# One layer of a hybrid encoder on one core: branch B's output chunks moved to the values' bank ring, a third home for its gates, finer key loads, and branch A's chunks with the rings swapped

## The chip, the core and the metric

The kernel runs on 1 core of one Trainium2 chip. A core has five engines that each follow an own list of instructions: TensorE (PE, with its weight loads shown as PEld), VectorE (DVE), ScalarE (ACT), GpSimd (POOL) and SyncE (SP, which here only issues DMAs). The metric is the device time of one execution in microseconds. The kernel before was run three times: 1937.47, 1938.02 and 1940.12 us, median 1938.02 us.

## The reference, cut to what matters

```python
D_MODEL = 1024; SEQ = 1024; HEAD_DIM = 64; NA_HEADS = 8; NB_HEADS = 8; NB_KV_HEADS = 2
GRID_W = 64; NA_KH_MAX = 8; NA_KW = 16; WIN = 128; BLOCK = 128; D_FF = 2816

h = x + 0.5 * swiglu(rms_norm(x, ffn1_norm), w_gate1, w_up1, w_down1)
u = rms_norm(h, mix_norm)
qA, kA, vA, qB, kB, vB, gA, gB = jnp.split(u @ w_in, SPLITS, axis=-1)
yA = neighbourhood_attention_2d(qA, kA, vA, na_rpb)                # 8 heads of 64
yB = windowed_gqa_sink(rope(qB), rope(kB), vB, sink_logit)         # 8 heads, 2 key heads
h = h + (sigmoid(gA) * (yA @ w_branch_a) + sigmoid(gB) * (yB @ w_branch_b)) @ w_out
h = h + 0.5 * swiglu(rms_norm(h, ffn2_norm), w_gate2, w_up2, w_down2)
out = rms_norm(h, final_norm)                                      # all float32
```

The line that the change touches is the sum of the two gated branches, and the attention that feeds it. `yA` and `yB` are 1024 tokens by 512; each branch's product with its 512x1024 weight is made in eight chunks of 128 output columns, transposed, so that a chunk is 128 partitions by 1024 tokens: two PSUM banks of 128x512. The gates `gA` and `gB` are likewise eight chunks of 128x1024 each.

## The kernel before, in words

**The whole.** In order of time: the first FFN, the input projection, an attention stage, the product with `w_out` (called the merge here), the second FFN, the last norm. Every float32 product with 512 columns is three TensorE matmuls in reduced precision, made by `mm3` (high part by high part, high by low, low by high: L149, L151 and L153), from operands that were split into a high part by an ACT cast (L95) and a low part by a DVE subtraction (L98).

**The attention stage** is a software pipeline over 64 units (`scores`, `turn`, `values`, lines 1364 to 1420). Units n = 0 to 31 are branch B (8 query blocks by 4 pairs of heads), units 32 to 63 are branch A (4 pairs of heads `hp` by 8 query blocks `j`). In step n the PE does the scores of unit n (L1379, L1380, two banks), the transposes of unit n-1's probabilities (L1398, two banks) and the product with the values of unit n-2 (L1412 for A, L1417 for B, one bank). Between them DVE and ACT make the softmax (L1382 on DVE, which also takes the score's bank out of PSUM; L1385, L1390 on ACT), the split of the transposed probabilities (L95, L98), and `write`, which takes the values' bank out of PSUM (L1348 copy on ACT; L1349 and twice L1352 on DVE).

**The bank rings.** PSUM has 8 banks here, in two rings of four: ring d (scores, transposes, transposes of V) and ring g (values, and the filling work below). A tile that asks a ring for a bank gets one that is or first becomes free.

**The filling work.** Twice per step, `filling(n)` takes some steps of a generator `filler()` and so puts other matmuls between those of attention: first ten projections of gate chunks (`gate`, 8 steps each, two banks of ring g, copied out by ACT at L1208 and stored to HBM, `g_d`, by POOL at L1209), then `branch_b`, the eight chunks of branch B's product (4 steps of 6 matmuls each), then the first two chunks of branch A (`branch_a`); branch A's other chunks follow after the last unit. A chunk's two banks come from ring d for even and ring g for odd chunks in branch B, and the other way round in branch A. Some 1.7 steps are taken per unit up to unit 45, 1.6 up to 59, and 3 after.

**The gates' way.** A chunk of branch B needs its gate back from `g_d`: SP fetches it (`fetch_gate`, L1245, 512 KB) into a tile of tag `xs`, of which there are two; ACT opens it (`open_gate`, L1254, one tanh over 128x1024, fixed in its place in ACT's order by `pin`); DVE evicts the chunk's two banks (L1279, twice 128x512) with the gate as the other operand. The gate of chunk dc+1 is asked for after the first step of chunk dc and opened at the end of chunk dc. The chunk's weights come by `fetch_w` (L1249, 512 KB) into a ring of tiles `ws`. The inputs `yB` come back from HBM by `fetch_y` (L1222) and are split in two by `split_y` (ACT and DVE, 128x1024, L95 and L98), four of them, during the steps of the last gate projection.

**Branch A's loads.** `prep_a(hp)` loads a pair of heads: per k two K tiles in high and low part, and the queries, by POOL (L1172, L1174, 256 KB each), then V by SP (L1177), and, some steps later, V's transposes (L1185, ring d) with their split into `fx`. It goes on by one `yield` at two places of each unit. The bias tables come by SP (L1157), the inner ones into parts of `fa`, the edge ones into `held[0..3]`, four of six tiles `hs`; `held[4]` and `held[5]` are not used. After blocks 3 and 7 of a pair of heads, POOL stores its `y` to `y_d` (L1357, 128x512), except for the last pair.

**The end of the stage.** After the last unit, branch A's chunks are evicted (L1518), added to branch B's (L1519), combined and stored (`combine`, L1495), and `Down(4, wo)`, the merge, begins: its first product takes the four banks of ring d, the second those of ring g.

**The order** of each engine's instructions is made when the kernel is built, by a scheduler that follows the program and its own estimate of durations; on the chip each engine takes its list in order and waits at semaphores. A DMA on SP or POOL that waits holds up those behind it.

## Time and profile before

| | us |
|---|---|
| median of 3 runs | 1938.02 (1937.47 to 1940.12) |
| the profiled execution | 1936.38 |
| its span, first to last instruction | 1934.6 |
| PE busy | 1916.3 (99%) |
| DVE busy | 1451.0 (75%) |
| ACT busy | 945.4 (49%) |
| POOL busy | 295.6 (15%) |
| granted TensorE clock, mean | 0.997 |

The profile comes from one profiled execution. Views of it that are used below: the page's head; the busy time of each engine in chosen stretches of time ("windows"); the chain of work that ended last, each piece with its start, its length and what it was; the waits, grouped by the engine and line that waited and what released it, with total, number and longest; the timeline of single instructions, where brackets give the idle time of the engine just before and what ended it; the groups of instructions of one line and shape, with number, total and mean; and the DMA issues with size and median time from issue to landing. `xs`, `ws`, `raw`, `fa`, `ar`, `fx` are tags of SBUF tiles, `d` and `g` the two rings of PSUM banks, `g_d`, `y_d`, `wab_d`, `zs_d`, `bm_d` tensors in HBM. On this time axis branch B's chunks run from 1081.33 us (first matmul) to 1170.46 us (end of the last eviction), and the merge's first matmul starts at 1213.43 us.

### The profile page before, as it was taken

To read this page: it belongs to the slowest core of one execution; us is meant where nothing else is said; L and a number is where in the kernel's file an instruction comes from. 1 tells how busy PE (TensorE), PEld (TensorE's weight loads), DVE (VectorE), ACT (ScalarE), POOL (GpSimd) and SP (SyncE) were. 2 spreads that over 40 slices of the span, in tenths; PEclk is the share of its full clock that TensorE was granted. 3 is DMA by queue.
4 is the path that set the end of the run, shared out by engine and by line. 5 is a ranking of instruction groups with operands and counts; after the bars stand their busy time and mean duration, and the time that the engine had idled before them with its cause. 6 is when DMAs were issued, how large, how long until landed. Compare 5 with 4: busy or idle time off the path is not lost.

```text
span 1934.6 us, 25628 instructions
## 1 busy us (share of the span) xinstructions
PE 1916.3 (99%) x8932; PEld 1597.9 (83%) x8932; DVE 1451.0 (75%) x2535; ACT 945.4 (49%) x1836; POOL 295.6 (15%) x454
## 2 busy tenths in 40 slices
PE   9999999999999999999999899999999999999998
PEld 7888888888888888888888788888888888888886
DVE  8987766768966878658778787989676566559864
ACT  7532444444446543447777774466333333344453
POOL 0011111214400112111122101010111001005210
PEclk9999999999999999999999999999999999999999
DMA  6254555586354267826357858443422323493341
GB/s 267 94 173 166 178 177 190 171 295 245 125 173 153 106 198 237 265 102 164 100 129 187 240 186 299 169 163 120 147 92 104 126 87 109 142 358 98 112 144 60
DMA packets 161344, 321.76 MB, mean 166 GB/s; under 512 B 16320, under 2 KB 69952, under 8 KB 161216
## 3 DMA queue, kind: packets, MB, share of 16 engines
q1 hardware_dynamic: 130048, 225.21, 35.8%
q0 software_dynamic: 30448, 93.87, 14.7%
q8 instruction: 70, 1.15, 0.2%
q10 hardware_dynamic: 720, 1.05, 0.1%
q14 instruction: 58, 0.48, 0.1%
HBM read 222.04 MB, written 99.81 MB: 166 GB/s over the span
## 4 chain that ended last, share of the span: by engine, by line
PE 95%; DVE 2%; ACT 1%; DMA 1%; issue 0%; SPq 0%; POOLq 0%; POOL 0%; DVEq 0%
PE g L149 17%; PE g L153 17%; PE g L151 17%; PE d L149 12%; PE d L153 12%; PE d L151 12%; PE d L1398 2%; PE g L1417 1%; PE d L1379 1%; PE d L1380 1%; PE g L1412 1%; DMA xs<-g_d 1%; PE d L142 1%; ACT fa L1385 0%; ACT ws L95 0%
## 5 line engine op out<-in xcount | busy, mean ns | idle before, releaser
L149 PE MATMUL g<-ar,ws 128*128 128x512 f32 x1096 | 414.8, 394 | 0.0
L151 PE MATMUL g<-ar,ws 128*128 128x512 f32 x1096 | 410.4, 390 | 0.0
L153 PE MATMUL g<-ar,ws 128*128 128x512 f32 x1096 | 409.6, 390 | 0.0
L149 PE MATMUL d<-ar,ws 128*128 128x512 f32 x760 | 293.2, 392 | 1.0 <-DVE nmx L1382 1.0
L151 PE MATMUL d<-ar,ws 128*128 128x512 f32 x760 | 292.9, 391 | 0.6 <-DVE ar L879 0.6
L153 PE MATMUL d<-ar,ws 128*128 128x512 f32 x760 | 291.9, 390 | 0.0
L153 PEld LDWEIGHTS g<-ar,ws 128*128 128x128 f32 x1096 | 205.6, 188 | 43.2
L151 PEld LDWEIGHTS g<-ar,ws 128*128 128x128 f32 x1096 | 205.5, 188 | 42.6
L149 PEld LDWEIGHTS g<-ar,ws 128*128 128x128 f32 x1096 | 201.2, 188 | 36.6 <-DVE fa L997 0.4
L322 DVE TENSOR_TENSOR ws<-raw,ws 128x512 fp32r<-128x512 f32 x210 | 143.9, 691 | 88.9 <-ACT ws L319 87.8
L319 ACT CAST ws<-raw 128x512 fp32r<-128x512 f32 x210 | 129.1, 621 | 145.6 <-PE g L153 64.5
L151 PEld LDWEIGHTS d<-ar,ws 128*128 128x128 f32 x760 | 142.9, 188 | 30.2 <-DVE ar L879 1.2
L149 PEld LDWEIGHTS d<-ar,ws 128*128 128x128 f32 x760 | 142.3, 188 | 30.9 <-DVE nmx L1382 1.2
L153 PEld LDWEIGHTS d<-ar,ws 128*128 128x128 f32 x760 | 142.8, 188 | 29.6 <-DVE ws L322 0.4
L95 ACT CAST ws<-raw 128x512 fp32r<-128x512 f32 (+1 forms) x107 | 70.7, 660 | 123.1 <-PE d L153 59.8
L98 DVE TENSOR_TENSOR ws<-raw,ws 128x512 fp32r<-128x512 f32 (+1 forms) x107 | 85.1, 795 | 46.0 <-ACT ws L95 45.9
L426 POOL DMA_DIRECT2D hid<-fx x91 | 49.4, 543 | 373.6 <-DVE fx L486 245.7
L98 DVE TENSOR_TENSOR ws<-ar,ws 128x512 fp32r<-128x512 f32 x114 | 94.1, 832 | 15.7 <-ACT ws L95 15.7
L95 ACT CAST ar<-raw 128x512 fp32r<-128x512 f32 (+1 forms) x81 | 54.1, 671 | 84.0 <-PE g L151 51.4
L1385 ACT ACTIVATE fa<-fa,nmx 128x385 f32<-128x385 f32 (+3 forms) x128 | 75.5, 591 | 33.7 <-DVE nmx L1382 32.0
L149 PE MATMUL g<-ws,ws 128*128 128x512 f32 x232 | 90.9, 392 | 0.0
L153 PE MATMUL g<-ws,ws 128*128 128x512 f32 x232 | 90.4, 390 | 0.0
(313 smaller groups left out, 3666.4 us busy)
## 6 DMA issues: line engine op xcount, KB each, us to landing
raw<-hid SPq DMA_DIRECT2D x70, 512.0 KB
hid<-fx POOLq DMA_DIRECT2D x91, 256.0 KB, 2.6
ar<-in_ffn_w_down_dram SPq DMA_DIRECT2D x32, 512.0 KB
raw<-in_ffn_w_up_dram SPq DMA_DIRECT2D x31, 512.0 KB
raw<-in_ffn_w_gate_dram SPq DMA_DIRECT2D x27, 512.0 KB
hid<-fa POOLq DMA_DIRECT2D x51, 256.0 KB, 2.7
raw<-in_w_in_dram SPq DMA_DIRECT2D x25, 512.0 KB
ar<-zs_d POOLq DMA_DIRECT2D x48, 256.0 KB, 7.0
```

The source lines that it names most:

```text
L95: hi = nc.scalar.copy(dst_hi, src)
L98: (eng or nc.vector).tensor_tensor(dst_lo, src, f32v(dst_hi), op=ALU.subtract)
L142: nc.tensor.transpose(pt[:, c * P:(c + 1) * P], xs[:, (half * 4 + c) * P:(half * 4 + c + 1) * P], ident)
L149: nc.tensor.matmul(b, lhs[0], r[0], start=first, stop=False, **kw)
L151: nc.tensor.matmul(b, lhs[0], r[1], start=False, stop=False, **kw)
L153: nc.tensor.matmul(b, lhs[1], r[0], start=False, stop=last, **kw)
L319: nc.scalar.copy(w[0][:, :512], a)
L322: nc.vector.tensor_tensor(w[0][:, 512:], a, f32v(w[0][:, :512]), op=ALU.subtract)
L426: nc.gpsimd.dma_start(hid[PRODUCTS.index(p), i], src)
L1379: nc.tensor.matmul(b[:, :nw], un["q"][s], un["kd"][s][:, k0 * P:k1 * P], start=True, stop=False)
L1385: nc.scalar.activation(pr, pr, AF.Exp, scale=-1.0, bias=nmx[:, s:s + 1], accum_out=ssum[:, s:s + 1])
L1398: nc.tensor.transpose(pt[:, i * P:(i + 1) * P], un["pr"][s][:, i * P:(i + 1) * P], ident)
```

## The change

It has six parts, all in the attention stage and the chunks beside it.

1. `branch_b` takes all its banks from ring g; before, its even chunks took ring d.
2. `branch_a` starts with ring d and goes on alternating, so its last chunk has its banks in ring g; before, in ring d.
3. The gates of branch B have three homes instead of two: gates 0, 3 and 6 go into `held[4]` and `held[5]`, in two DMAs of 128x512; the others into `xs`. A gate is asked for two chunks ahead (after the first step of chunk dc that of chunk dc+2, for chunk 0 after its third step); gates 0 and 1 are asked for during the last gate projection, at its steps 0 and 5. The tanh is two instructions of 128x512 per gate.
4. The third `split_y` of `yB` moves from step 5 to step 6 of the last gate projection, the fourth from step 6 of it into chunk 0, after its first step.
5. `prep_a` has one more `yield` after each of its four groups of K loads, so a pair of heads takes 13 steps of the generator instead of 9, and the transposes of V come two units later.
6. For the first three pairs of heads, `write` of branch A makes both heads' sum in one DVE instruction of 64x2x128 instead of two of 64x128, so `y` lies in 64 partitions with the two heads side by side, and is stored as 64x2x512.

The number of PE matmuls stays at 8932. DVE has 24 instructions fewer, ACT 8 more, SP 3 DMAs more.

```diff
             for lo, dst in enumerate((kd, kl)):
                 for a in halves(dst[k]):
                     nc.gpsimd.dma_start(a, head(k, 4, lo))
+                yield
...
     def branch_a(i):

-        bs = [bank("gd"[i % 2]) for _ in range(2)]
+        bs = [bank("dg"[i % 2]) for _ in range(2)]
...
     def fetch_gate(dc):
-        mix["rb", dc] = xs4()
-        nc.sync.dma_start(mix["rb", dc], g_d[D + dc * P:D + (dc + 1) * P, :])
+        t = xs4() if dc % 3 else None
+        mix["rb", dc] = [held[4 + k] if t is None else t[:, k * 512:k * 512 + 512] for k in range(2)]
+        for r, cols in zip(mix["rb", dc] if t is None else [t], (slice(0, 512), slice(512, 1024)) if t is None else (slice(0, 1024),)):
+            nc.sync.dma_start(r, g_d[D + dc * P:D + (dc + 1) * P, cols])
...
     def open_gate(dc):
-        r = mix["rb", dc]
-        pin(nc.scalar.activation(r, r, AF.Tanh, scale=0.5))
+        for r in mix["rb", dc]:
+            pin(nc.scalar.activation(r, r, AF.Tanh, scale=0.5))
...
         for dc in range(NC8):
-            bs = [bank("dg"[dc % 2]) for _ in range(2)]
+            bs = [bank("g") for _ in range(2)]
             mm = branch_mm(bs, mix.pop(("w", dc)), Y_B)
             for c in range(4):
                 drain(mm, 1)
                 yield
-                if c == 0:
+                if c == (0 if dc else 2) and dc + 2 < NC8:
+                    fetch_gate(dc + 2)
+                if c == 0 and dc == 0:
+                    split_y(Y_B[3], 3 * P, nc.vector)
+                if c == 1:
                     if dc == 0:
                         open_gate(0)
-                    if dc + 1 < NC8:
-                        fetch_gate(dc + 1)
-                elif c == 1:
                     fetch_w(dc + 2)
                 elif c == 3 and dc + 1 < NC8:
                     open_gate(dc + 1)
...
-                yield from gate(dc, {0: lambda: [fetch_y(c * P) for c in range(2)],
+                yield from gate(dc, {0: lambda: [fetch_gate(0)] + [fetch_y(c * P) for c in range(2)],
                                      1: lambda: fetch_w(0),
                                      2: lambda: fetch_y(2 * P),
                                      3: lambda: split_y(Y_B[0], 0, nc.vector),
                                      4: lambda: [split_y(Y_B[1], P, nc.vector), fetch_y(3 * P)],
-                                     5: lambda: [split_y(Y_B[2], 2 * P, nc.vector), fetch_gate(0)],
-                                     6: lambda: split_y(Y_B[3], 3 * P, nc.vector)})
+                                     5: lambda: fetch_gate(1),
+                                     6: lambda: split_y(Y_B[2], 2 * P, nc.vector)})
...
                     cols = slice((j - 3) * P, (j + 1) * P)
-                    if j in (3, 7) and hp == 3:
+                    if hp < 3:
+                        both = y[j // 4 * HD:j // 4 * HD + HD].rearrange("p (s t) -> p s t", s=2)
+                        nc.vector.tensor_tensor(both[:, :, j % 4 * P:(j % 4 + 1) * P], o[:HD, :, 0, :], lo, op=ALU.add)
+                        if j in (3, 7):
+                            nc.gpsimd.dma_start(y_d[512 + hp * P:512 + (hp + 1) * P, cols].rearrange("(s p) t -> p s t", s=2), both)
+                        return
```

Four places of the built order show it. The lines of the changed file are three to eight higher than those of the file before: the gates' fetch is L1245 before and L1248 after, the weights' L1249 and L1252, the `y` fetch L1222 and L1223, the tanh L1254 and L1257, the eviction of branch B L1279 and L1283, that of branch A L1518 and L1526, the transposes L1398 and L1406, the scores L1379, L1380 and L1387, L1388, ACT's part of the softmax L1385, L1390 and L1393, L1398, the copy of the values L1348 and L1352.

The first place is SP's list around branch B's first chunks. Before, `xs_9574` is gate 1, `xs_9711` gate 2, `xs_9856` gate 3, and `ws_9596`, `ws_9747` and `ws_9889` are the weights of chunks 2, 3 and 4:

```order
L1245 DMA xs_9574<-g_d 128x1024
L1157 DMA hs_6979<-bm_d 128x384
L1249 DMA ws_9596<-wab_d 128x1024
L1157 DMA hs_6980<-bm_d 128x384
L1249 DMA ws_9747<-wab_d 128x1024
L1245 DMA xs_9711<-g_d 128x1024
L1245 DMA xs_9856<-g_d 128x1024
L1222 DMA raw_10168<-y_d 128x1024
L1249 DMA ws_9889<-wab_d 128x1024
```

After, `xs_9630` is gate 2, the pair `hs_6981`, `hs_6982` (which are `held[4]` and `held[5]`) is gate 3, `xs_9843` gate 4, and `ws_9584`, `ws_9727`, `ws_9865` are the weights of chunks 2, 3 and 4:

```order
L1157 DMA hs_6979<-bm_d 128x384
L1157 DMA hs_6980<-bm_d 128x384
L1223 DMA raw_10092<-y_d 128x1024
L1248 DMA xs_9630<-g_d 128x1024
L1252 DMA ws_9584<-wab_d 128x1024
L1248 DMA hs_6981<-g_d 128x512
L1248 DMA hs_6982<-g_d 128x512
L1252 DMA ws_9727<-wab_d 128x1024
L1223 DMA raw_10152<-y_d 128x1024
L1248 DMA xs_9843<-g_d 128x1024
L1252 DMA ws_9865<-wab_d 128x1024
```

Gate 2 now stands ahead of the weights of chunk 2; the pair of gate 3, which goes where gate 0 was and so waits for chunk 0's eviction, stands ahead of the weights of chunk 3, which stood ahead of that wait before.

The second place is the PE's list where chunk 0 ends and chunk 1 begins. Before, chunk 0 is `d_9538`, `d_9539`, chunk 1 `g_9685`, `g_9686`, and `g_9649` is a unit's values:

```order
L153 MATMUL d_9538<-ar_5004,ws_9320 128x512
L1398 MATMUL d_9638<-ident,fa 128x128 x2
L153 MATMUL d_9539<-ar_5004,ws_9320 128x512
L1412 MATMUL g_9649<-ws_9582,fx_8927 128x256 x3
L1412 MATMUL g_9649<-ws_9583,fx_8928 128x256 x3
L1379 MATMUL d_9663<-ar_5003 128x384
L1380 MATMUL d_9663<-ar_563,ar_5003 128x384
L149 MATMUL g_9685<-ar_4625,ws_9536 128x512
L1379 MATMUL d_9668<-ar_5003 128x384
L1380 MATMUL d_9668<-ar_563,ar_5003 128x384
L149 MATMUL g_9686<-ar_4625,ws_9536 128x512
L151 MATMUL g_9685<-ar_4625,ws_9536 128x512
```

After, chunk 0 is `g_9517`, `g_9518`, chunk 1 `g_9670`, `g_9671`, and `g_9638` is a unit's values:

```order
L153 MATMUL g_9518<-ar_5004,ws_9309 128x512
L1420 MATMUL g_9638<-ws_9569,fx_9031 128x256 x3
L1387 MATMUL d_9651<-ar_5003 128x384
L1388 MATMUL d_9651<-ar_563,ar_5003 128x384
L149 MATMUL g_9670<-ar_4625,ws_9515 128x512
L151 MATMUL g_9670<-ar_4625,ws_9515 128x512
L1387 MATMUL d_9656<-ar_5003 128x384
L1388 MATMUL d_9656<-ar_563,ar_5003 128x384
L153 MATMUL g_9670<-ar_4625,ws_9515 128x512
L149 MATMUL g_9670<-ar_4625,ws_9515 128x512
L151 MATMUL g_9670<-ar_4625,ws_9515 128x512
L153 MATMUL g_9670<-ar_4625,ws_9515 128x512
```

Both chunks and the values are now in ring g, and chunk 1 runs ahead in its first bank; its second bank, `g_9671`, begins six rows further down, after one more matmul in the first and a unit's transposes.

The third place is ACT's list around the copies of the last gate projection's banks. Before, `fx_9400` is a cast of a V transpose of the third pair of heads, `ar_5004` the high parts of the last two splits of `yB`, `xs_9530` the gate that is copied out:

```order
L95 CAST fx_9400<-d_9447 128x4x64
L95 CAST ar_5004<-raw_9342 128x8x8x16
L1390 ACTIVATE fa<-fa,rc_9433 128x384
L95 CAST ws_9516<-d_9518 128x3x128
L1208 COPY xs_9530<-g_9231 128x512
L95 CAST ws_9517<-d_9524 128x3x128
L1208 COPY xs_9530<-g_9232 128x512
L1348 COPY s_771_6976<-g_9546 64x256
L1385 ACTIVATE fa,ssum_9493<-fa,nmx_9492 128x384 x2
L1390 ACTIVATE fa<-fa,rc_9494 128x384
L95 CAST ar_5004<-raw_9412 128x8x8x16
```

After, the copies of the last gate are a few rows ahead of this piece, and `raw_9333`, `raw_9393` are the third and fourth block of `yB`:

```order
L1398 ACTIVATE fa<-fa,rc_9462 128x384
L95 CAST ar_5004<-raw_9333 128x8x8x16
L95 CAST fx_9498<-d_9500 128x4x64
L1352 COPY s_771_6976<-g_9525 64x256
L1393 ACTIVATE fa,ssum_9536<-fa,nmx_9535 128x256 x2
L95 CAST fx_9498<-d_9551 128x4x64
L95 CAST fx_9499<-d_9500 128x4x64
L95 CAST ws_9568<-d_9570 128x3x128
L1398 ACTIVATE fa<-fa,rc_9537 128x256
L95 CAST fx_9499<-d_9551 128x4x64
L95 CAST ar_5004<-raw_9393 128x8x8x16
L95 CAST ws_9569<-d_9576 128x3x128
```

The third split of `yB` and the four casts of V, which stood ahead of the gate's copies, now stand behind them, among the work beside chunk 0. Each of these casts has a subtraction (L98) on DVE that follows it.

The fourth place is DVE's last evictions of branch A, chunks 6 and 7. Before:

```order
L1518 SCALAR_TENSOR_TENSOR raw_10753<-raw_10753,g_10829 128x512
L1518 SCALAR_TENSOR_TENSOR raw_10753<-raw_10753,g_10830 128x512
L1519 TENSOR_TENSOR ar_9534<-ar_9534,raw_10753 128x1024
L1495 TENSOR_TENSOR fa<-ar_9534 128x512
L1518 SCALAR_TENSOR_TENSOR raw_10788<-raw_10788,d_10860 128x512
L1518 SCALAR_TENSOR_TENSOR raw_10788<-raw_10788,d_10861 128x512
L1519 TENSOR_TENSOR ar_9535<-ar_9535,raw_10788 128x1024
```

After:

```order
L1526 SCALAR_TENSOR_TENSOR raw_10737<-raw_10737,d_10813 128x512
L1526 SCALAR_TENSOR_TENSOR raw_10737<-raw_10737,d_10814 128x512
L1527 TENSOR_TENSOR ar_9513<-ar_9513,raw_10737 128x1024
L1503 TENSOR_TENSOR fa<-ar_9513 128x512
L1526 SCALAR_TENSOR_TENSOR raw_10772<-raw_10772,g_10844 128x512
L1526 SCALAR_TENSOR_TENSOR raw_10772<-raw_10772,g_10845 128x512
L1527 TENSOR_TENSOR ar_9514<-ar_9514,raw_10772 128x1024
```

The last chunk's banks are now in ring g; those of ring d, which the merge takes first, are evicted one chunk earlier.

7 lines of the change are left out of this document (3 added, 4 removed).

## The prediction

> **What bounds the kernel.** I read the page's head first, then the chain of work that ended last, the waits, and stretches of the attention stage.
>
> ```profile
> span 1934.6 us, 25628 instructions
> PE 1916.3 (99%) x8932; PEld 1597.9 (83%) x8932; DVE 1451.0 (75%) x2535; ACT 945.4 (49%) x1836; POOL 295.6 (15%) x454
> ```
>
> PE is busy 1916.3 of 1934.6 us, and the change leaves its 8932 matmuls alone. So it can gain only from the 18.3 us in which PE idles, from matmuls that run at a lower clock, and from those that last longer than need be. The idle time by its causes, PE's waits first, then those of ACT and SP within 1030 to 1215 us:
>
> ```profile
> PE d L1398 <- DVE nmx L1382: 6.4, 1, 6.4
> PE d L149 <- DVE raw L1518: 1.1, 1, 1.1
> PE d L149 <- DVE nmx L1382: 1.0, 1, 1.0
> ACT xs L1254 <- DMA xs<-g_d: 7.0, 1, 7.0
> SPq L1245 <- DVE ar L1279: 26.2, 4, 9.3
> ```
>
> Three single waits of PE stand in the stretch that the change touches, 8.5 us of the 18.3. The longest belongs to a chain, here with start and length of each piece:
>
> ```profile
> 1094.60 14.76 DMA xs<-g_d
> 1109.39 1.06 ACT xs L1254
> 1110.44 0.51 ACT fa L1390
> 1112.32 0.90 PE d L1398 x3
> ```
>
> The timeline shows how the DMA came to be late:
>
> ```profile
> 1085.59 0.32 SPq L1245 DMA_DIRECT2D xs<-g_d  x1
> 1090.45 0.32 SPq L1249 DMA_DIRECT2D ws<-wab_d  x1
> 1093.86 0.67 DVE L1279 SCALAR_TENSOR_TENSOR ar<-xs,d 128x512 f32<-128x512 f32 x1
> 1094.50 1.05 ACT L1254 ACTIVATE xs<-xs 128x1024 f32<-128x1024 f32 x1
> 1094.60 10.02 SPq L1245 DMA_DIRECT2D xs<-g_d  x2
> 1109.39 1.06 ACT L1254 ACTIVATE xs<-xs 128x1024 f32<-128x1024 f32 x1 [6.99 <-DMA xs<-g_d]
> 1112.32 0.90 PE L1398 MATMUL d<-ident,fa 128*128 128x128 f32 x3 [6.45 <-DVE nmx L1382]
> ```
>
> Gate 1 (issued at 1085.59) was in before its tanh at 1094.50, which waited for nothing. Gate 2 could go only when DVE had evicted chunk 0 (1093.86 + 0.67) and so freed the tile; it needed 14.76 us. Its tanh is pinned in ACT's order, so the softmax of the next unit stood behind it: ACT idled 6.99 us, PE 6.45 us. The stretches around it:
>
> ```profile
> core 0: us, PE busy (x) PEld busy (x) DVE busy (x) ACT busy (x) POOL busy (x), PEclk, DMA share, GB/s
> 1069.00:1081.30 12.30, 11.20 (x71) 9.40 (x69) 10.90 (x28) 10.97 (x25) 0.00 (x0) 1.00 0.63 213
> 1081.30:1093.20 11.90, 11.87 (x69) 10.03 (x69) 11.02 (x39) 10.78 (x28) 5.83 (x11) 1.00 0.94 253
> 1093.20:1105.90 12.70, 12.67 (x71) 10.70 (x69) 10.24 (x30) 7.96 (x21) 2.12 (x4) 1.00 1.23 277
> 1105.90:1115.60 9.70, 3.28 (x11) 2.75 (x12) 3.09 (x10) 4.15 (x10) 0.00 (x0) 0.65 0.60 223
> 880.00:1020.00 140.00, 139.84 (x822) 122.86 (x821) 106.94 (x337) 109.63 (x285) 21.60 (x39) 1.00 0.50 126
> ```
>
> In the fourth stretch the granted clock is 0.65, and PE's 3.28 us there, all behind the stall, did about half of what such a time does elsewhere: a second price of the same stall.
>
> **The gains.** (1) Gate 2 is now asked for two chunks ahead, into the tile from which the last gate projection was stored, and on SP ahead of chunk 2's weights: about where gate 1's fetch stood, 1085.6 to 1088. Even with the 14.76 us of the slow one it lands by 1103; ACT reached the tanh at 1109.39 - 6.99 = 1102.4. So the 6.45 us go, and with them half of the 3.28 us, 1.6, of which I count 1.5: together 7.95, taken whole. What is late next is priced below. (2) Branch A's last chunk now has its banks in ring g. The merge's first product, in ring d, waited 1.13 us for that chunk's eviction:
>
> ```profile
> 1212.17 1.28 DVE L1518 SCALAR_TENSOR_TENSOR raw<-raw,g 128x512 f32<-128x512 f32 x2
> 1215.36 1.28 DVE L1518 SCALAR_TENSOR_TENSOR raw<-raw,d 128x512 f32<-128x512 f32 x2
> 1216.09 0.50 PE L149 MATMUL d<-ws,ws 128*128 128x512 f32 x1 [1.13 <-DVE raw L1518]
> ```
>
> Chunk 6, which has ring d now, is evicted at 1212.17, 3.2 us before chunk 7, so d is free in time; the second product takes g much later. Gain 1.13 (0 at least). (3) Chunk 0's first bank in ring d waited 1.00 us for a unit's scores to be taken out:
>
> ```profile
> 1081.33 0.50 PE L149 MATMUL d<-ar,ws 128*128 128x512 f32 x1 [1.00 <-DVE nmx L1382]
> ```
>
> In ring g it waits for the last gate's copies instead, which now stand earlier on ACT. Gain 1.00, at least 0. Sum of gains: 7.95 + 1.13 + 1.00 = 10.1.
>
> **The costs.** The groups of instructions within 1020 to 1170 us give the durations, and the DMA issues within 1040 to 1180 us the landings:
>
> ```profile
> L95 ACT CAST fx<-d 128x256 fp32r<-128x256 f32 x12 | 4.5, 375 | 1.4 <-DVE fx L98 0.9 <-PE d L1185 0.4
> L98 DVE TENSOR_TENSOR fx<-d,fx 128x256 fp32r<-128x256 f32 x12 | 5.0, 420 | 0.5 <-ACT fx L95 0.4
> L95 ACT CAST ar<-raw 128x1024 fp32r<-128x1024 f32 x7 | 7.3, 1048 | 0.0
> L98 DVE TENSOR_TENSOR ar<-raw,ar 128x1024 fp32r<-128x1024 f32 x7 | 8.6, 1225 | 1.5 <-ACT ar L95 1.3
> L1279 DVE SCALAR_TENSOR_TENSOR ar<-xs,g 128x512 f32<-128x512 f32 x8 | 5.4, 675 | 0.0
> L1208 ACT COPY xs<-g 128x512 f32<-128x512 f32 x6 | 3.6, 597 | 0.2 <-PE g L153 0.2
> L1352 DVE TENSOR_TENSOR fa<-g,s 64x128 f32<-64x128 f32 x58 | 16.3, 281 | 0.4
> L1349 DVE TENSOR_TENSOR s<-g,s 64x256 f32<-64x256 f32 x29 | 11.9, 410 | 7.3 <-ACT s L1348 7.2
> ar<-zs_d POOLq DMA_DIRECT2D x24, 256.0 KB, 12.9
> y_d<-fa POOLq DMA_DIRECT2D x6, 256.0 KB, 3.7
> ```
>
> (4) Work that moves into chunk 0: four casts and subtractions of V (ACT 4 x 0.375 = 1.5, DVE 4 x 0.42 = 1.7) and the third split of yB (ACT 1.05, DVE 1.23). In the stretch of chunk 0, 1081.30 to 1093.20, ACT then has 10.78 + 2.55 = 13.3 and DVE 11.02 + 2.9 = 13.9 us to do in 11.9. The overhang is 1.4 to 2.0 us. Some passes to the next stretch, where ACT has 4.7 and DVE 2.5 us free; PE is in ACT's and DVE's hands in the softmax, so some shows. Bounds 0 and 2.9 (DVE's whole addition); I take the middle, 1.5.
>
> (5) Ring g for all chunks. Two of its four banks belong to a chunk, two to the values. At each of the seven passages from one chunk to the next the new chunk must take the values' two banks, and the next values wait for the old chunk's evictions, 0.675 us each. Bounds: nothing, or both evictions whole, 1.36 us per passage. The nearest row is 880 to 1020 us, where gates (two banks of ring g each) follow each other beside branch B's values: 139.84 of 140.00 us busy, several passages at next to no price. There the eviction is ACT's, and here DVE's, which is the fuller engine in the third stretch (10.24 against 7.96); I take 0.25 each, 1.7.
>
> (6) The rest at nothing. The eight tanh as 16: by ACT's copy of 128x512, 0.597, against the tanh of 1.05 over 128x1024, the two halves take 0.14 more, 1.1 for all eight; ACT has 4.7 us free in the third stretch, and without that cover the 1.1 us would show. DVE's 24 instructions fewer: per unit 0.410 (64x256 in one) in place of 2 x 0.281, 0.15 x 24 = 3.7 us off DVE, off the path. The y store from 64 partitions: nearest rows 3.7 us (128 partitions) and 12.9 us (the 64-partition key loads); its reader, the fetch of y on SP, comes units later, and if it came sooner, SP's weights would wait behind it. On POOL this store now stands among the next pair's key loads and holds those behind it until its last block is written. The key loads spread over six yields, three units, where they took one unit: the count of L1349 makes a unit 150 / 29 = 5.2 us, and the pair's first scores stand four units behind the last load, 21 us against 12.9 to landing; without this cover those scores would wait. SP's 3 more DMAs: 0.32 us each on an engine that issues nothing else.
>
> (7) What could be late next, with the evictions of chunks 0 and 1 on the timeline:
>
> ```profile
> 1093.18 0.69 DVE L1279 SCALAR_TENSOR_TENSOR ar<-xs,d 128x512 f32<-128x512 f32 x1
> 1102.15 0.67 DVE L1279 SCALAR_TENSOR_TENSOR ar<-xs,g 128x512 f32<-128x512 f32 x1
> ```
>
> It is SP's order. Gate 3's pair waits for chunk 0's eviction, as gate 2's did, so is issued near 1094.6. With 14.76 us it lands at 1109.4. Chunk 3's weights stand behind it, while before they left at 1090.45; 512 KB at the third stretch's 277 GB/s are another 1.9 us, so about 1111.3. The need: evictions of chunks 0 and 1 were 9 us apart (1093.18 and 1102.15), so without the stall chunk 3 starts and gate 3 opens at about 1112. That is 1 to 3 us of margin. I count 0; a delay would cost PE its length, and, if it is long like the stall above, the clock behind it too.
>
> The sum: -10.1 + 1.5 + 1.7 = -6.9. The profiled execution took 1936.38 us, so 1929.5; the median of the runs stands 1.64 above it (1938.02), which gives 1931.1, and I say 1931.
>
> **Rivals.** *Bank waits.* If each of the seven passages shows both evictions, the cost of (5) is 9.5 instead of 1.7: 1936.38 - 10.1 + 1.5 + 9.5 = 1937.3, 1938.9 on the runs' scale, no change. For it speaks the third stretch's full DVE; against it the gates' stretch, and that PE's order runs the new chunk's first bank ahead while the second is still taken. The Trainium skill, page "Perfetto Trace Analysis", section "Matmuls" (under "Optimizing Tensor Performance"), has a rule on this side: independent groups of matmuls are to rotate through different banks, so that the eviction of one lies beside the next one's matmuls; by it, two rings for the chunks were better than one, and the time would be this rival's. The gates' stretch of this trace does not bear it out for a ring of four with two spare banks.
>
> *The stall shrinks but does not go.* Gate 3 or chunk 3's weights are 1 to 3 us late, or chunk 0's overhang shows whole (2.9): gains of 3 to 5, about 1934. For it speaks the margin of 1 to 3 us; against it that the key loads no longer crowd before 1097, and that the DMA share falls to 0.60 behind 1106.
>
> *SP's queue makes a new stall, and the kernel is slower.* Chunk 3's weights now stand on SP behind a fetch that waits for an eviction. To use up the 6.9 us and pass 0.2% (3.9 us), PE must wait about 9 us with 1.5 for the clock: weights landing at 1121 or later, 26 us from 1094.6 against the 14.76 measured. Then PE idles 10 or more us at chunk 3: 1931 + 12 = 1943. For it: the third stretch's DMA share of 1.23 is the fullest of them, and the y fetch and key loads are added there. Against: the bytes in all are the same.
>
> **How the numbers follow.** My case has 0.63, bank waits 0.13, the shrunken stall 0.15, SP's queue 0.09. About 0.2%, 3.9 us, is what a measurement of this kernel can tell from no change: below 1934.1 is faster, above 1941.9 slower. Faster: 0.63 and most of the shrunken stall, 0.74. Same: the bank waits and the rest, 0.17. Slower: 0.09. The low end takes (4) and (5) near nothing: 1938.02 - 10.1 = 1927.9, a little lower for DVE's relief, 1927. The high end covers the shrunken stall and half of the bank waits, 1937; what is left out is SP's queue and the rest of the bank waits, and a little below.
>
> **What would show it.** Right: the wait of L1257 for `xs<-g_d` gone, no PE wait above 1 us between 1080 and 1170 us, the clock 1.00 throughout, the merge without its 1.1 us wait, PE's span to the merge 7 us shorter. Step (4) is wrong if chunk 0's stretch is longer by more than 2.9 or not at all; (5) if PE shows waits for L1283, or values later at each passage; (7) if ACT waits for `hs<-g_d` or PE for `ws<-wab_d` at chunk 3. The forecast fails if SP's waiting pair holds up the weights, or if the order that comes out of the ring leaves DVE and ACT no time in the softmax.

## The result, and the profile after

The changed kernel takes 1933.79 us, the median of 7 runs (1932.19 to 1934.91), beside 1939.43 us for the kernel before in the 7 runs that go with them (1937.47 to 1941.24). The ratio is 0.9971, with a 95% interval of 0.9959 to 0.9982: 5.6 us or 0.3% faster, 3.5 to 8.0 by the interval. The forecast was 1931 (1927 to 1937). The profiled executions differ by less, 1936.38 and 1932.98, 3.4 us; the traces compared below are those two.

The head of the page, and the waits of PE over the whole program (total, number, longest):

```profile
span 1931.0 us, 25634 instructions
PE 1915.4 (99%) x8932; PEld 1598.1 (83%) x8932; DVE 1447.1 (75%) x2511; ACT 944.3 (49%) x1844; POOL 296.5 (15%) x454
```

```profile
PE g L149 <- DMA ws<-wab_d: 4.4, 1, 4.4
PE g L798 <- POOL ident masks.py:199: 1.5, 1, 1.5
PE d L153 <- DVE ws L322: 0.9, 1, 0.9
```

The wait of 6.45 us for the softmax is gone, and so are the two waits for banks, 1.13 and 1.00. A new one of 4.4 us stands near the place of the first: a matmul waits for weights. The second row is in the kernel before too; the third lies behind the merge, at 1313.78 us, is new, and nothing here says what makes it.

The chain of waits of the changed kernel leads to that matmul (start, length, what):

```profile
1079.48 6.94 DMA g_d<-xs
...
1086.49 0.32 SPq L1248
...
1086.85 17.44 DMA ws<-wab_d
...
1104.42 0.77 PE g L149
```

And SP's own timeline from the last y fetch to gate 3:

```profile
1079.85 0.90 SPq L1252 DMA_DIRECT2D ws<-wab_d  x1
1082.28 0.86 SPq L1157 DMA_DIRECT2D hs<-bm_d  x2
1083.31 0.37 SPq L1223 DMA_DIRECT2D raw<-y_d  x1
1086.49 0.32 SPq L1248 DMA_DIRECT2D xs<-g_d  x1
1086.85 0.65 SPq L1252 DMA_DIRECT2D ws<-wab_d  x1
1094.55 0.80 SPq L1248 DMA_DIRECT2D hs<-g_d  x2
1095.45 0.38 SPq L1252 DMA_DIRECT2D ws<-wab_d  x1
```

At 1086.49 us SP issues gate 2, which had to wait until the last gate's store had left the same tile (6.94 us from 1079.48). Chunk 2's weights, asked for at 1086.85 behind a y fetch of 512 KB and that gate, land 17.44 us later, at 1104.29. PE stood ready for them at 1104.42 - 4.39 = 1100.03. The stretches show what that did, first two slices of ten microseconds over the stall, then the 4.6 us behind it, then three longer ones, for which the kernel before had 43.42, 60.00 and 58.87 us of PE at clocks of 0.93, 1.00 and 1.00:

```profile
core 0: us, PE busy (x) PEld busy (x) DVE busy (x) ACT busy (x) POOL busy (x), PEclk, DMA share, GB/s
1090.00:1100.00 10.00, 9.96 (x55) 8.15 (x53) 9.24 (x31) 8.32 (x24) 2.77 (x5) 1.00 1.24 271
1100.00:1110.00 10.00, 5.61 (x27) 4.82 (x27) 4.34 (x12) 4.20 (x11) 0.00 (x0) 0.83 1.09 299
1104.42:1109.00 4.58, 4.58 (x21) 3.92 (x22) 1.52 (x4) 2.28 (x6) 0.00 (x0) 0.69 1.13 293
1069.00:1120.00 51.00, 46.36 (x270) 39.78 (x268) 40.76 (x117) 38.86 (x100) 8.71 (x16) 0.97 0.83 225
1120.00:1180.00 60.00, 59.90 (x335) 51.43 (x333) 47.31 (x132) 42.89 (x105) 0.77 (x2) 1.00 0.65 229
1180.00:1240.00 60.00, 60.00 (x266) 49.68 (x265) 55.53 (x83) 20.94 (x34) 8.73 (x16) 1.00 0.66 237
```

Behind the stall the granted clock is 0.69 for 4.6 us, so the new stall has a second price like that of the old one: by an estimate from this row, 0.31 of 4.58 us, 1.4 us. The DMA share is above 1 from 1090 on, in both kernels (1.22 and 1.01 in the first two slices before).

Where the time went, by events that both traces have. Rows of the kernel before, DVE's evictions of chunks 3 and 7 and the merge's first matmul:

```profile
1132.24 0.67 DVE L1279 SCALAR_TENSOR_TENSOR ar<-xs,g 128x512 f32<-128x512 f32 x1
1168.93 0.67 DVE L1279 SCALAR_TENSOR_TENSOR ar<-xs,g 128x512 f32<-128x512 f32 x1
1213.43 0.39 PE L149 MATMUL d<-ws,ws 128*128 128x512 f32 x1
```

The changed kernel, chunks 0, 3 and 7 and the merge:

```profile
1093.49 1.28 DVE L1283 SCALAR_TENSOR_TENSOR ar<-hs,g 128x512 f32<-128x512 f32 x2
1128.70 0.68 DVE L1283 SCALAR_TENSOR_TENSOR ar<-hs,g 128x512 f32<-128x512 f32 x1
1166.49 1.28 DVE L1283 SCALAR_TENSOR_TENSOR ar<-xs,g 128x512 f32<-128x512 f32 x2
1210.63 0.39 PE L149 MATMUL d<-ws,ws 128*128 128x512 f32 x1
```

Chunk 0 starts to be evicted 0.3 us later than before (1093.18), chunk 3 3.5 us earlier, chunk 7 2.4, the merge begins 2.8 earlier, and its wait of 1.1 no longer follows. So the way from chunk 0 to chunk 3 is 3.9 us shorter, that from chunk 3 to chunk 7 1.1 longer, that from there to the merge 0.4 shorter, and the merge gave 1.1 more. The first two of these also hold moved work: by the windows between the same events, up to chunk 3 there are 180 matmuls where there were 187, from there to chunk 7 211 where there were 207. Some records can be missing, but in that second stretch PE is busy throughout at full clock in both kernels, so the 1.1 is not a wait. By the waits alone the stall gave 2.1 us (6.45 to 4.39), chunk 0's bank 1.0 and the merge's 1.1.

### The profile page after: what moved, and what is told of

Read it like the earlier page. It is cut to its first block, busy times and chain, and to the rows that moved or that the text cites. A ratio compares the mean times of both kernels' runs of the same rounds, so it can differ in the third digit from the quotient of the medians.

```text
span 1931.0 us, 25634 instructions
## 1 busy us (share of the span) xinstructions
PE 1915.4 (99%) x8932; PEld 1598.1 (83%) x8932; DVE 1447.1 (75%) x2511; ACT 944.3 (49%) x1844; POOL 296.5 (15%) x454
## 4 chain that ended last, share of the span: by engine, by line
PE 93%; DVE 2%; DMA 2%; issue 1%; ACT 1%; POOL 0%; SPq 0%; POOLq 0%; DVEq 0%; ACTq 0%
PE g L149 17%; PE g L151 17%; PE g L153 17%; PE d L153 12%; PE d L149 12%; PE d L151 12%; PE d L1406 2%; PE g L1425 1%; DMA ws<-wab_d 1%; PE d L1387 1%; PE d L1388 1%; PE g L1420 1%; DVE ar L98 1%; PE d L142 0%; DMA g_d<-xs 0%
## 5 line engine op out<-in xcount | busy, mean ns | idle before, releaser
L149 PE MATMUL g<-ar,ws 128*128 128x512 f32 x1128 | 426.5, 395 | 4.4 <-DMA ws<-wab_d 4.4
L151 PE MATMUL g<-ar,ws 128*128 128x512 f32 x1128 | 421.0, 391 | 0.0
L153 PE MATMUL g<-ar,ws 128*128 128x512 f32 x1128 | 420.3, 390 | 0.0
L149 PE MATMUL d<-ar,ws 128*128 128x512 f32 x728 | 282.0, 391 | 0.5 <-ACT ar L877 0.5
L153 PE MATMUL d<-ar,ws 128*128 128x512 f32 x728 | 281.0, 389 | 0.9 <-DVE ws L322 0.9
L151 PE MATMUL d<-ar,ws 128*128 128x512 f32 x728 | 281.1, 389 | 0.6 <-DVE ar L879 0.6
L153 PEld LDWEIGHTS g<-ar,ws 128*128 128x128 f32 x1128 | 211.8, 188 | 44.8
L151 PEld LDWEIGHTS g<-ar,ws 128*128 128x128 f32 x1128 | 211.7, 188 | 44.1 <-DVE ar L98 0.2
L149 PEld LDWEIGHTS g<-ar,ws 128*128 128x128 f32 x1128 | 206.9, 188 | 41.5 <-issue 5.0
L149 PEld LDWEIGHTS d<-ar,ws 128*128 128x128 f32 x728 | 136.6, 188 | 29.9 <-ACT ar L877 1.1
L153 PEld LDWEIGHTS d<-ar,ws 128*128 128x128 f32 x728 | 136.7, 188 | 29.6 <-DVE ws L322 1.4
L151 PEld LDWEIGHTS d<-ar,ws 128*128 128x128 f32 x728 | 136.7, 188 | 29.3 <-DVE ar L879 1.2
L98 DVE TENSOR_TENSOR ws<-raw,ws 128x512 fp32r<-128x512 f32 (+1 forms) x107 | 85.1, 796 | 47.7 <-ACT ws L95 47.6
L98 DVE TENSOR_TENSOR ws<-ar,ws 128x512 fp32r<-128x512 f32 x114 | 93.8, 830 | 14.1 <-ACT ws L95 14.1
L1393 ACT ACTIVATE fa<-fa,nmx 128x385 f32<-128x385 f32 (+3 forms) x128 | 75.4, 590 | 33.1 <-DVE nmx L1390 31.9
```

The costliest lines, as they stand in the source:

```text
L98: (eng or nc.vector).tensor_tensor(dst_lo, src, f32v(dst_hi), op=ALU.subtract)
L149: nc.tensor.matmul(b, lhs[0], r[0], start=first, stop=False, **kw)
L151: nc.tensor.matmul(b, lhs[0], r[1], start=False, stop=False, **kw)
L153: nc.tensor.matmul(b, lhs[1], r[0], start=False, stop=last, **kw)
L1393: nc.scalar.activation(pr, pr, AF.Exp, scale=-1.0, bias=nmx[:, s:s + 1], accum_out=ssum[:, s:s + 1])
```

## The experiments

My theory from these views: the gain is the gate's stall, and what was lost of it went to chunk 2's weights, which came late because of their place on SP and, through part 5, the y fetch ahead of them. Rivals: the bytes asked for between 1080 and 1105 us are too many whatever their order; the rings are the gain, or a loss. The experiments ran in three sets, each on one chip with its own runs of the kernel before (medians 1937.73, 1938.69 and 1939.19 us); ratios are to those. The first four below are the first set, the next four the second, the last three the third.

**The rings alone (parts 1 and 2 on the kernel before).**

```diff
-            bs = [bank("dg"[dc % 2]) for _ in range(2)]
+            bs = [bank("g") for _ in range(2)]
...
-        bs = [bank("gd"[i % 2]) for _ in range(2)]
+        bs = [bank("dg"[i % 2]) for _ in range(2)]
```

> The kernel before with parts 1 and 2 alone: branch B's chunks in ring g, branch A's rings swapped; gates, loads and writes as before. My theory: the gate stall is a matter of the gates' homes, so ACT still waits some 7 us for gate 2 and PE some 6.4; the merge's wait of 1.1 us goes (the changed kernel gained 1.5 us there), the seven passages cost some 1.2 us. Net 0 to -1.5 us against the kernel before. Rival (the rings are the gain): 3 us or more faster than before. Rival (the rings are a loss): 5 or more slower.

Measured: 1933.42 us against 1937.73, ratio 0.9975 (0.9963 to 0.9986). My theory fell here: the rings alone are worth 4.3 us by the medians. Yet the reason isn't what the rival has it to be. PE's waits between 1000 and 1240 us, ACT's waits for gates, and POOL's key loads in that trace:

```profile
PE g L149 <- DMA ws<-wab_d: 4.3, 1, 4.3
```

```profile
1097.18 1.06 ACT L1254 ACTIVATE xs<-xs 128x1024 f32<-128x1024 f32 x1 [1.29 <-DMA xs<-g_d]
1109.32 1.06 ACT L1254 ACTIVATE xs<-xs 128x1024 f32<-128x1024 f32 x1 [1.69 <-DMA xs<-g_d]
```

```profile
1091.02 0.51 POOL L1174 DMA_DIRECT2D ar<-zs_d  x1 [0.51 <-DMA ar<-zs_d]
1093.02 0.51 POOL L1174 DMA_DIRECT2D ar<-zs_d  x1 [1.49 <-DMA ar<-zs_d]
```

Gate 2 is as late as before (its tanh at 1109.32, before at 1109.39), but now PE stops earlier, for chunk 2's weights. Its stop of 4.3 us takes the place of the one of 6.45, and by its end the gate is nearly there: ACT waits 1.7 us instead of 7.0. The last key loads went out 3.5 and 4.4 us earlier than in the kernel before (1094.50 and 1097.40 there), into the time in which the weights were under way, which came in time there. So gate and weights share one burst of transfers, and either can be its last. How much of the 4.3 us is the shorter stop, and how much the clock and the bank waits, these runs don't separate.

**The gates alone (parts 3 and 4 on the kernel before; of the edit only the main lines).**

```diff
+        t = xs4() if dc % 3 else None
+        mix["rb", dc] = [held[4 + k] if t is None else t[:, k * 512:k * 512 + 512] for k in range(2)]
...
+                if c == (0 if dc else 2) and dc + 2 < NC8:
+                    fetch_gate(dc + 2)
```

> The kernel before with parts 3 and 4 alone: the gates' three homes, asked for two chunks ahead, and the two splits moved; rings, key loads and the write as before. My theory: nearly the whole gain is here. ACT's wait for a gate goes (7.0 us before); the y fetch stays at about 1076 us, so the burst of transfers behind 1080 us is 512 KB lighter than in the changed kernel and chunk 2's weights come in with a wait of 0 to 2.5 us instead of 4.4. The merge's wait of 1.1 stays. 4 to 7 us faster than before. Rival (the transfers as a whole are the limit, whatever their order): again a wait of 4 us or more at chunk 2 or 3, 1 to 3 us faster than before.

Measured: 1933.18 us (1929.03 to 1935.17), ratio 0.9967 (0.9954 to 0.9979). PE's waits between 1000 and 1240 us:

```profile
PE d L149 <- DMA ws<-wab_d: 3.4, 1, 3.4
PE d L149 <- DVE raw L1521: 1.2, 1, 1.2
```

4.6 us faster, with no wait of ACT for a gate, and the merge's wait still there, as expected; the wait for weights is 3.4, above the 0 to 2.5 that I gave. With either half of the change the time is the changed kernel's within the scatter: the halves don't add up, since both run into chunk 2's weights. Here the weights are late though the y fetch went out at 1077.29 us, about as early as in the kernel before.

**Without part 5 (key loads in two steps).**

```diff
                     nc.gpsimd.dma_start(a, head(k, 4, lo))
-                yield
```

> The changed kernel without part 5 (the key loads again in two steps, V's transposes two units earlier). Theory: part 5 made the new stall, since the later transposes keep the tile into which branch A's first y is fetched, and so moved that fetch from 1076 us, where the DMA engines were a third busy, to 1083, in the burst; without it chunk 2's weights wait 0 to 2.5 us instead of 4.4: 2 to 5 us faster than the changed kernel. Rival (SP's order: gate 2 waits for the last gate's store ahead of the weights): the wait stays at 4 us or more, within 1 us of the changed kernel.

Measured: 1930.26 us (1927.59 to 1931.44), ratio 0.9953 (0.9941 to 0.9966). The y fetch is back ahead of the burst, and the wait shrinks. From SP's timeline, and PE's waits:

```profile
1078.23 0.32 SPq L1222 DMA_DIRECT2D raw<-y_d  x1
```

```profile
PE g L149 <- DMA ws<-wab_d: 2.9, 1, 2.9
```

The medians are 3.5 us apart, but stem from different sets of runs and chips; set against the runs of before in each, the difference is 1.8 (7.5 against 5.6 us of gain), and the intervals of the ratios overlap. So part 5 costs the changed kernel some 2 to 3.5 us by these figures. The wait gives 1.5 of that (4.4 to 2.9). The clock adds the 1.4 estimated above, for behind this shorter stop it stayed at full speed:

```profile
1105.09:1109.67 4.58, 4.58 (x25) 4.02 (x26) 1.32 (x6) 0.68 (x2) 0.00 (x0) 1.00 0.97 375
```

Two things move with part 5: V's transposes and with them the y fetch, which goes out 5.1 us earlier here, and POOL's twelve key loads, which go out from 1083.74 to 1094.9 us in place of 1081.44 to 1099.0. This run does not separate them. As 2.9 us of wait stay here, and 3.4 with the gates alone, the y fetch is at most a part of the cause.

**Weights earlier.** The weights of chunks 1 and 2 are asked for at the last step of the last gate projection, the later ones a chunk earlier.

```diff
+                                     7: lambda: [fetch_w(1), fetch_w(2)],
...
-        fetch_w(1)
...
-                    fetch_w(dc + 2)
+                    if dc + 3 < NC8 + 2:
+                        fetch_w(dc + 3)
```

> The changed kernel, with the weights of chunks 1 and 2 asked for at the last step of the last gate projection and those of the later chunks one chunk earlier, so that on SP chunk 2's weights stand right behind chunk 1's and ahead of gate 2. Theory that SP's order makes the new stall (chunk 2's weights behind a y fetch and a gate that waits): the wait of 4.4 us goes and no other takes its place; 4 to 6 us faster than the changed kernel, about 1928. Rival, that the bytes asked for between 1080 and 1105 us are too many whatever the order: a wait of 3 us or more turns up for gate 2, gate 3 or chunk 3's weights, and the time is within 1.5 us of the changed kernel's.

Measured: 1925.93 us (1925.53 to 1926.26), ratio 0.9933 (0.9921 to 0.9946): 11.8 us faster than the kernel before, and within the scatter the fastest kernel of this study. Against the changed kernel it is 7.9 us by the medians, where 4 to 6 had been expected; the wait and its clock, 4.4 and an estimated 1.4, explain 5.8. The burst and the stall's stretch:

```profile
1069.00:1120.00 51.00, 50.75 (x308) 44.18 (x306) 45.50 (x133) 44.64 (x115) 8.62 (x16) 1.00 0.91 252
```

PE is busy 50.75 of 51.00 us at full clock, while the DMA engines move more in this stretch than in the changed kernel (252 against 225 GB/s). The rival of too many bytes falls: order suffices. The runs are also closer together, 0.7 us from lowest to highest where the changed kernel has 2.7; but part 2 undone (below), where no transfer is late either, has 3.0, so that the late transfer is what varies is not shown.

**Chunk 2's weights alone.** On the changed kernel, only this fetch is moved:

```diff
         fetch_w(1)
+        fetch_w(2)
...
-                    fetch_w(dc + 2)
+                    if dc:
+                        fetch_w(dc + 2)
```

> The changed kernel with one fetch moved: chunk 2's weights are asked for right behind chunk 1's, ahead of gate 2 and the y fetch; all other fetches stay, so chunk 3's weights still stand behind gate 3, which waits for chunk 0's eviction. If the prediction's step (7) has its margin (gate 3 and chunk 3's weights land 1 to 3 us before they are needed), no wait above 1 us is left and the time is about that of the kernel with all weights earlier, 1926. If the margin is not there, PE or ACT waits 1 to 4 us at chunk 3 and the time is 1928 to 1932.

Measured: 1926.35 us (1925.77 to 1927.49), ratio 0.9939 (0.9926 to 0.9951). PE has no wait above 0.2 us between 1000 and 1240 us, and ACT none for a gate. Chunk 3's weights, still behind the waiting gate 3, come in time. From SP's timeline, the weights of chunks 1 and 2, gate 2 and the y fetch:

```profile
1079.33 1.36 SPq L1252 DMA_DIRECT2D ws<-wab_d  x2
1085.82 0.32 SPq L1248 DMA_DIRECT2D xs<-g_d  x1
1086.75 0.36 SPq L1223 DMA_DIRECT2D raw<-y_d  x1
```

The edit moves one fetch, which goes out some 6 us earlier, and the built order that came of it also has the y fetch behind gate 2. With that the time is the fastest kernel's within the scatter.

**Weights earlier on the kernel before.** The same edit as for the fastest kernel, without the change.

> The kernel before with the weights alone earlier, as in the faster version; gates, rings, key loads and write as before. Theory that two late transfers share the stretch and that the gates' homes are needed too: gate 2 still goes out only behind chunk 0's eviction, so ACT waits 5 to 8 us for it and PE 4 to 7, and the time is within 2 us of the kernel before. Rival, that the order of the weights alone was the matter: PE's waits in the stretch fall below 2 us and it is 5 us or more faster than before.

Measured: 1936.66 us (1935.46 to 1938.82) against 1938.69, ratio 0.9993 (0.9984 to 1.0002): no difference clear of the scatter. The tanh of gates 1 and 2, and PE's waits between 1000 and 1240 us:

```profile
1099.77 1.06 ACT L1254 ACTIVATE xs<-xs 128x1024 f32<-128x1024 f32 x1 [4.19 <-DMA xs<-g_d]
1112.12 1.06 ACT L1254 ACTIVATE xs<-xs 128x1024 f32<-128x1024 f32 x1 [5.27 <-DMA xs<-g_d]
```

```profile
PE d L1399 <- DVE nmx L1383: 4.8, 1, 4.8
PE d L1380 <- DVE nmx L1383: 2.4, 1, 2.4
```

With the weights ahead, the gates are last: gate 1 now waits as well. Neither order helps as long as gate 2 can only leave behind chunk 0's eviction. Both parts, an early home and the place of the weights, are needed for a stretch without a stall. No run has these two and nothing else of the change, and none has the gates' third home without the earlier asking; the next ones undo the other parts one by one.

**Single parts on the quiet kernel.** The remaining five start from the kernel with weights earlier, called quiet here because no transfer is late in it, and undo one part each. They ran on two other chips than that kernel did, so each is compared with the others of its set.

Part 1 undone, even chunks in ring d again:

```diff
-            bs = [bank("g") for _ in range(2)]
+            bs = [bank("dg"[dc % 2]) for _ in range(2)]
```

> The changed kernel with weights earlier (1925.9 us, its runs within 0.8 us), with part 1 undone: branch B's even chunks in ring d again. The price of the passages in ring g by itself. Step (5) of the prediction had 1.7 us for ring g; by it this is 1 to 2 us faster than 1925.9, less the wait for a bank of ring d at chunk 0 (1.0 in the kernel before): -1 to +0.5. Rival, that ring g costs nothing or gains: 0.5 to 3 us slower.

Part 5 undone (the edit as above):

> The changed kernel with weights earlier (1925.9 us), with part 5 undone. Without the stall the earlier y fetch has nothing to mend, so if part 5 cost the changed kernel its 3 us only by the late transfer, this is within 1 us of 1925.9. If the transposes' later place costs or gains by itself, 1.5 us or more to one side.

Measured on one chip: part 1 undone 1927.78 us (1927.07 to 1927.99; ratio 0.9944, 0.9930 to 0.9957), part 5 undone 1926.06 (1925.37 to 1926.21; ratio 0.9935, 0.9922 to 0.9947). Part 5 undone differs by 0.1 us from the quiet kernel's 1925.93 on the other chip, so part 5 shows no cost once nothing is late. Ring g, which I had costed at 1.7 us, is 1.7 us faster than two rings against the run with part 5 undone, and 1.4 against chunk 2's weights alone (1926.35), whose runs overlap with its. PE's only wait in the stretch with two rings is at chunk 0, for a bank of ring d whose transposes are not yet split:

```profile
1088.10 0.55 PE L1407 MATMUL d<-ident,fa 128*128 128x128 f32 x3 [1.50 <-DVE ws L98]
```

Part 2, part 4 and part 6 undone:

```diff
-        bs = [bank("dg"[i % 2]) for _ in range(2)]
+        bs = [bank("gd"[i % 2]) for _ in range(2)]
```

> The changed kernel with weights earlier (1925.9 us), with part 2 undone: branch A's last chunk has its banks in ring d again. Step (2) of the prediction had 1.13 us for it: the wait of the merge's first product comes back with 1 to 1.2 us, and the time is 1 to 1.5 us longer. Rival, that it is bought back before the second FFN begins: within 0.5 us.

```diff
-                if c == 0 and dc == 0:
-                    split_y(Y_B[3], 3 * P, nc.vector)
...
-                                     5: lambda: fetch_gate(1),
-                                     6: lambda: split_y(Y_B[2], 2 * P, nc.vector)})
+                                     5: lambda: [split_y(Y_B[2], 2 * P, nc.vector), fetch_gate(1)],
+                                     6: lambda: split_y(Y_B[3], 3 * P, nc.vector)})
```

> The changed kernel with weights earlier (1925.9 us), with part 4 undone: the third and fourth split of yB at steps 5 and 6 of the last gate projection again. Step (4) of the prediction had 1.5 us (0 to 2.9) for moving work into chunk 0; if it is paid there and not saved ahead of it, this is 0.5 to 1.5 us faster. Rival, that the work costs the same in either place: within 0.5 us. Rival, that it is worse ahead of chunk 0, where ACT was busy 10.97 of 12.3 us: 0.5 to 2 us slower.

```diff
-                    if hp < 3:
-                        both = y[j // 4 * HD:j // 4 * HD + HD].rearrange("p (s t) -> p s t", s=2)
-                        nc.vector.tensor_tensor(both[:, :, j % 4 * P:(j % 4 + 1) * P], o[:HD, :, 0, :], lo, op=ALU.add)
...
+                    for s in range(2):
+                        rows = slice(s * HD, s * HD + HD)
+                        nc.vector.tensor_tensor(y[rows, j * P:(j + 1) * P], o[:HD, s, 0, :], lo[:, s, :], op=ALU.add)
```

> The changed kernel with weights earlier (1925.9 us), with part 6 undone: two sums of 64x128 on DVE for each unit of branch A again, y stored from 128 partitions. Step (6) of the prediction put the 3.7 us of DVE at nothing: within 0.5 us. Rival, that DVE's time shows in the softmax: 1 to 3.7 us slower.

Measured on one chip: part 2 undone 1926.59 us (1925.63 to 1928.61; ratio 0.9934, 0.9922 to 0.9946), part 4 undone 1927.37 (1926.64 to 1928.70; 0.9937, 0.9924 to 0.9949), part 6 undone 1925.56 (1925.29 to 1926.82; 0.9930, 0.9917 to 0.9942). Part 6 is worth nothing, as costed. Part 2 is worth 1.0 us at most here, by medians whose ranges overlap (against part 6 undone). Its trace shows no wait of the merge: DVE came to the last chunk's eviction 0.8 us behind the merge's first matmul, where it came 1.9 behind it in the kernel before:

```profile
1204.04 0.39 PE L149 MATMUL d<-ws,ws 128*128 128x512 f32 x1
1204.88 1.28 DVE L1527 SCALAR_TENSOR_TENSOR raw<-raw,d 128x512 f32<-128x512 f32 x2
```

Part 4 undone looks slower, by 1.8 us against part 6 undone (the ranges overlap by 0.2) and by 0.8 against part 2 undone, which no sum of busy time had told. The trace, that of its slowest run, has a cause. With the splits ahead of the last gate's second copy on ACT, that copy is made at 1084.45 (1078.49 in the kernel with weights earlier) and stored behind it; SP, which wants the tile for gate 2, waits for the store and issues gate 2 at 1094.44 instead of 1086.33, and the tanh waits:

```profile
1084.45 0.60 ACT L1209 COPY xs<-g 128x512 f32<-128x512 f32 x1
1105.18 1.15 ACT L1257 ACTIVATE xs<-xs 128x512 f32<-128x512 f32 x2 [1.48 <-DMA xs<-g_d]
```

## Why the prediction was right, and where it was not

The time lies in the range and the change of 5.6 us is near the 6.9 forecast, but part of that is two errors that offset each other. Of the signs that the prediction set for being right, two came, no wait for the gate and no wait of the merge. Three did not: PE waited 4.4 us in the stretch, the clock fell to 0.69, and the merge began 2.8 us earlier instead of 7.

Step (1), the gate: right in its mechanism. No tanh waits for a gate in the changed kernel; the trace's semaphore updates have gate 2 landed at 1101.32 us, where the forecast had 1103 at the latest. Its size, 7.95 taken whole, was wrong: the wait shrank by 2.1 us, and the clock's price came back.

Step (7), what is late next, is the step that failed. It asked the question at chunk 3 and found a margin of 1 to 3 us; there the margin held, as the run with chunk 2's weights alone shows. It did not ask it at chunk 2. Step (1) counted gate 2's place ahead of chunk 2's weights as a gain, and (7) never took up that these weights had been in just in time before. In the trace of before SP issues them at 1086.48 us and PE uses them at 1101.19, with no wait:

```profile
1086.48 0.61 SPq L1249 DMA_DIRECT2D ws<-wab_d  x1
1101.19 0.70 PE L149 MATMUL d<-ar,ws 128*128 128x512 f32 x2
```

The updates of the semaphore by which this transfer reports are complete at 1101.06, 0.13 us ahead of the matmul: there was no margin. In the changed kernel the weights landed 3.2 us later (1104.29), and PE came for them 1.2 us earlier (1100.03); together these are the 4.4 us, with a clock of 0.69 behind them. The lateness is not a matter of gate 2's place alone: it stands on SP where gate 1 stood before, with the same 512 KB. New ahead of the weights are the y fetch of 512 KB and the second of two bias tables (192 KB), and POOL's key loads begin 2.4 us earlier (1081.44 against 1083.87). With the rings alone SP's list is the old one, and the weights are late all the same. How the 3.2 us divide among these stays open; that an earlier place on SP mends it is shown.

This is what the rival of the shrunken stall has, a late transfer of weights that leaves a gain of 3 to 5 and a time of about 1934 (1933.79 was measured), at another chunk than it named and with a chance of 0.15; my own case, with 0.63, did not come about as it was told.

Step (2), the merge's bank: 1.13 forecast; the wait is gone and the stretch 1180 to 1240 us has 1.13 us more of PE (60.00 against 58.87). Right in this kernel; on the quiet kernel it is worth less.

Steps (3) and (4), the start of chunk 0: +0.5 net forecast, 0.3 measured at its eviction. But (4) by itself may have the wrong sign: the moved splits free the last gate's tile earlier, and to move them back costs 0.8 to 1.8 us on the quiet kernel, by runs that overlap. The step counted ACT's and DVE's time and not what stands behind them on SP.

Step (5), ring g: 1.7 us forecast for the seven passages. In the changed kernel PE was busy 59.90 of 60.00 us from 1120 to 1180, so the passages there cost next to nothing; on the quiet kernel the ring is 1.4 to 1.7 us better than two rings, where a bank wait of 1.50 in ring d at chunk 0 shows, of the kind that I had counted under (3) at 1.0. The rival of bank waits falls. The rule that was quoted for it, from the Trainium skill's page "Perfetto Trace Analysis", section "Matmuls", is kept by four banks of one ring as well: of the two arrangements, the one with more rings was the slower.

Step (6), the rest at nothing: right for the write; the halves of the tanh wait for nothing in the trace, and no run tests them alone. For the key loads it was wrong by some 2 to 3.5 us, what the run without part 5 gained: it asked whether the loads come in time, and not what their new place does to the transfers beside them, nor did it price V's transposes, which the two added units of delay carry with them, and the y fetch behind these. The order of SP, quoted with the change, shows that fetch one row ahead of gate 2, where before it went out at 1076.23 us, ahead of the whole burst.

By the waits and the clock the gains came to some 4.4 us instead of 10.1, and the costs to some 0.5 instead of 3.2: up to the merge, its wait taken in, the two traces are 3.9 us apart, not 6.9. The answer came out within the range for a reason in part other than the one given, and with luck: the two profiled executions alone show half of the forecast. Why the medians differ by 5.6 us and the two profiled executions by 3.4 stays open; the profiled one of the kernel before, 1936.38, was faster than each of its seven runs (1937.47 at least), and that kernel alone ran between 1936.29 and 1943.56 us in these studies.

## What to carry to other kernels

When a late transfer is found, ask of every transfer in the same burst when it was needed, not only of the one that was late: the next in line may have had no margin at all (0.13 us here), and whatever is put ahead of it or beside it, or brings its reader forward, makes it the new stall. Write the burst down in the order of issue, with the time at which each is used, and sort it by that time; here, on top of the change, one fetch of 512 KB asked for some six microseconds earlier was worth as much as the six parts of the change together, while on the kernel before the earlier weights gave nothing clear of the scatter. A delay that looks free (one more yield) should be followed to the tiles that it keeps busy and to the queue that waits for them.

## What was not expected of the hardware

A 512 KB transfer took 17.44 us to land in the burst, with the DMA share at 1.03 to 1.24, where a store of 512 KB issued 7.4 us ahead of it took 6.94. Transfers on SP and POOL share that burst: in the run with the rings alone the last two key loads, which POOL issued some 4 us earlier, went along with weights of SP that were 4.3 us late. In the changed kernel the y fetch, gate 2 and chunk 2's weights, all on SP, landed in the order of their issue, at 1097.78, 1101.32 and 1104.29 us, and key loads of POOL landed between them, at 1100.16, 1101.92 and 1103.76. The Trainium skill, page "DMA: Bandwidth & Descriptors", section "Queues, rings and completion order", says that each DMA engine takes turns between the queues that have work for it, a packet at a time, and takes the descriptors of one queue in order. The trace agrees with that.

The granted clock fell behind some stops of PE and not behind others. In the 4.58 us that follow it was 0.66 behind the 6.45 us of the kernel before, 0.69 behind the 4.39 of the changed kernel and 0.63 behind the 3.40 with the gates alone, but 1.00 behind the 2.88 without part 5. So among these runs the shortest stop cost its own length and no more.
